# A fused LoRA kernel whose ScalarE copies B's rows on a semaphore of their own

## The chip, the core and the metric

The kernel runs on one core of one Trainium2 chip. The time is device microseconds of one execution, and each kernel's figure is the median of several executions. The engines of the core are TensorE (PE in the profile, with its weight loads as PEld), VectorE (DVE), ScalarE (ACT), GpSimd (POOL) and SyncE (SP), which here issues all transfers. Each engine works through its own program in order, and they meet only through semaphores: counters that one instruction raises and another waits for.

## The reference

```
x: 16 x 512 x 768 float32,  A: 768 x 16,  B: 16 x 768,  scale = 0.5
lora = np.matmul(np.matmul(x, A), B)
return (x + scale * lora).astype(np.float32)
```

x is 8192 rows of 768 numbers, 24 MB; the result is as large. A and B are small. The two products need little arithmetic, so most of what the kernel does is to bring x in, turn it so that TensorE can contract over the 768 columns, add the product, and bring the sum out.

## The kernel before, in words

The 8192 rows make 64 tiles of 128 rows, held on the chip as float32 in x_sb (48 tiles fit at once). They come in eight loads of 2, 6, 8, 8, 8, 16, 8 and 8 tiles and go out in five stores of 8, 8, 16, 16 and 16 tiles. Compute goes by **groups of eight tiles**, eight groups in all (g = 0 to 7). For each group:

- *Cast* (`narrowed`, line 196): x is copied to float16 into xn, the first four tiles of a group by ScalarE and the last four by GpSimd. Group 0 is cut finer: GpSimd casts its first two tiles, ScalarE the next two and then the last four. Before a cast an engine waits for the load that brought its tiles (lines 190 to 193) and for xn to be free again (line 195).
- *Turn* (`turned`, line 256): VectorE transposes xn in 32 x 32 blocks into xt.
- *Project* (`projected`, line 286): 24 matmuls of TensorE multiply xt with w_bd, the blocks of A, into the PSUM tile y_ps. The first lowers s_turned, the second raises **s_taken** (xt and xn of this group have been taken), the last raises s_y.
- *Spread* (line 241): ScalarE multiplies y_ps by the scale and writes it as four diagonal blocks into y_bd. The first of the four raises s_narrow, as the casts do; the last raises s_spread.
- *Raise* (`raised`, line 307): for each of the four pairs of tiles TensorE multiplies y_bd with b_mm, the rows of B, into one of the two PSUM tiles lora_ps, and raises s_lora.
- *Add* (`summed`, line 261): VectorE adds the lora_ps tile onto x_sb, in place. The stores take x_sb from there.

Casts and turns run a group ahead: during group g's raises, group g+1 is cast, turned and projected. TensorE's program has these groups as a loop (line 328); the other engines' programs are written out.

**B's rows** take a way of their own at the start. SyncE loads them spread over the partitions into b_rows (line 160). GpSimd casts them to float16 (b_half, line 214). Two matmuls of line 320 with the selection matrix pick put each row in the partitions where the raise wants it, into the first of the lora_ps tiles. ScalarE copies it out of PSUM into b_mm (line 234) and raises s_bm, for which TensorE waits ahead of its loop (line 327).

The order around the change: TensorE runs the two matmuls of line 320, waits for w_bd and for group 0's turn, and projects group 0 (line 326). ScalarE casts its parts of group 0, **waits for s_taken to reach 1** (line 233), copies b_mm, and then takes group 1's cast. Since it has already waited for s_taken at 1, ScalarE's cast of group 1 waits only for the load: that is why line 194 has `g > (e is nc.scalar)`, which is g > 1 for ScalarE and g > 0 for GpSimd.

SyncE's order: the two first loads, A, B, four more loads (lines 161 and 162), then a wait for the first two groups' sums and for ten raises (line 170), then the first two stores (lines 171 and 172). The last two loads each wait for one of these stores, because they go where its tiles lay. The later stores wait for the sums of their parts, and the third also for a raise of the sixth group (line 182). Once the sums are done GpSimd clears the semaphores (line 349), and the last store is issued after that (line 356).

Of the kernel before, what the change touches and what calls it, by code (L numbers as in the profile page):

```python
# [28 lines left out]
def kernel(  # L29
# [8 lines left out]
    nc = tc.nc  # L38
# [44 lines left out]
    def sem(name):  # L83
        sems.append(nc.alloc_semaphore(name))
        return sems[-1]
# [10 lines left out]
    def memory(t2, i, s, n):  # L96
        S = PARTS[i]
        return t2[ds(parts[i], S * P), :].rearrange("(p s) d -> p s d", s=S)[:, ds(s, n), :]

    def held(i, s, n):  # L100
        return tiles(where.index((i, s)), n)

    def tiles(t, n):
        return x_all[:, ds(t % ROOM, n), :]
# [6 lines left out]
    def load_of(t):  # L111
        i, s = where[t]
        return next(k for k, ld in enumerate(LOADS) if ld[0] == i and ld[1] <= s < ld[1] + ld[2])
# [1 line left out]
    assert SETS * SET == NC  # L115
    s_a, s_b = sem("s_a"), sem("s_b")
    s_ready, s_brows, s_pick = sem("s_ready"), sem("s_brows"), sem("s_pick")
    s_w, s_bh, s_bm = sem("s_w"), sem("s_bh"), sem("s_bm")
    s_first, s_narrow, s_turned, s_taken = sem("s_first"), sem("s_narrow"), sem("s_turned"), sem("s_taken")
    s_y, s_spread, s_lora = sem("s_y"), sem("s_spread"), sem("s_lora")  # L120

# [66 lines left out]
    def narrowed(e, copy, g, first, n=SUB):  # L188
        t = g * GROUP + first
        for k in dict.fromkeys(load_of(t + k) for k in range(n)):  # L190
            if (e, k) not in here:
                here.add((e, k))
                e.wait_ge(s_load[k], 16)
        if g > (e is nc.scalar):
            e.wait_ge(s_taken, g)
        ins = copy(out=xn[:, ds(first, n), :], in_=tiles(t, n))  # L196

        ins.then_inc(s_narrow if g else s_first if first else s_a, 1)

    def on_gpsimd(e):  # L200
        e.memset(a_rows[0:Q], 0.0).then_inc(s_ready, 1)  # L201
        e.memset(b_rows, 0.0).then_inc(s_brows, 1)  # L202
        e.memset(pick, 0.0).then_inc(s_pick, 1)
        e.memset(w_bd.rearrange("p c k m -> p (c k m)").bitcast(fp32), 0.0)  # L204
        e.memset(y_bd.rearrange("p s m -> p (s m)").bitcast(fp32), 0.0).then_inc(s_ready, 1)  # L205
        e.wait_ge(s_pick, 1)
        e.affine_select(  # L207
            out=pick, in_=pick, compare_op=mybir.AluOpType.not_equal, fill=1.0, base=0,
            pattern=[[0, NQ], [-APART, Q]], channel_multiplier=1,
        ).then_inc(s_pick, 1)  # L210
        narrowed(e, e.tensor_copy, 0, 0, SUB // 2)
        e.wait_ge(s_pick, 2)
        e.wait_ge(s_b, 16)
        e.tensor_copy(out=b_half, in_=b_rows).then_inc(s_bh, 1)  # L214
        e.wait_ge(s_ready, 3)
        e.tensor_copy(  # L216
            out=w_one.rearrange("i (c e) k r -> i c e (k r)", c=SETS),
            in_=a_t[0:Q].rearrange("i k r (e c) -> i c e (k r)", c=SET)[:, 0:SETS, 0:SET, :],
        ).then_inc(s_w, 1)
        e.wait_ge(s_w, 1)  # L220
        for b in range(NQ):
            e.tensor_copy(  # L222
                out=w_bd[ds(b * Q, Q), :, :, ds(b * Q, R)], in_=w_one
            ).then_inc(s_w, 1)
            e.wait_ge(s_w, b + 2)
        for g in range(1, NG):
            narrowed(e, e.tensor_copy, g, SUB)

    def on_scalar(e):
        narrowed(e, e.copy, 0, SUB // 2, SUB // 2)  # L230
        narrowed(e, e.copy, 0, SUB)

        e.wait_ge(s_taken, 1)
        e.copy(out=b_mm, in_=lora[0][:, 0, :]).then_inc(s_bm, 1)  # L234
        for g in range(NG):
            if g + 1 < NG:
                narrowed(e, e.copy, g + 1, 0)
            e.wait_ge(s_y, g + 1)
            for b in range(NQ):
                q = ds(b * Q, Q)  # L240
                last = e.mul(out=y_bd[q, :, q], in_=y_ps[q, :, :], mul=sc)  # L241
                if b == 0 and g + 1 < NG:

                    last.then_inc(s_narrow, 1)
            last.then_inc(s_spread, 1)
# [32 lines left out]
    def on_tensor(e):  # L278


        xv = xt.rearrange("p s (c j k) -> p s c j k", c=NC, k=2)

        def projected(first, last):
            for m in range(first, last):
                c, k = divmod(m, 2)
                mm = e.matmul(  # L286
                    y_ps, w_bd[:, c, k, :], xv[:, :, c, :, k],
                    start=(m == 0), stop=(m == MMS - 1),
                )
                if m == 0:  # L290
                    mm.then_inc(s_turned, -1)
                if m == 1:

                    mm.then_inc(s_taken, 1)
                if m == MMS - 1:
                    mm.then_inc(s_y, 1)

        def raised(p):
            if p == 0:
                e.wait_ge(s_spread, 1)  # L300
            free = s_free[(p + 2) % PAIRS]
            e.wait_ge(free, 1)
            t = lora[p % 2]
            mms = []
            for k in range(2):
                for n0, w in ((0, 512), (512, 256)) if k == 0 else ((0, 256), (256, 512)):
                    mms.append(e.matmul(  # L307
                        t[:, k, ds(n0, w)], y_bd[:, 2 * p + k, :], b_mm[:, ds(n0, w)],
                        start=True, stop=True,
                    ))  # L310
            if p == 0:
                mms[0].then_inc(s_raise, 1)
                mms[2].then_inc(s_spread, -1)
            mms[1].then_inc(free, -1)
            mms[-1].then_inc(s_lora, 1)

        e.wait_ge(s_pick, 2)
        e.wait_ge(s_bh, 1)
        for n0, w in ((0, 512), (512, 256)):
            last = e.matmul(  # L320
                lora[0][:, 0, ds(n0, w)], pick.rearrange("p b r -> p (b r)"),
                b_half[:, ds(n0, w)], start=True, stop=True,
            )
        e.wait_ge(s_w, 1 + NQ)
        e.wait_ge(s_turned, 1)
        projected(0, MMS)
        e.wait_ge(s_bm, 1)
        with e.Fori(0, NG - 1):
            raised(0)
            raised(1)  # L330
            e.wait_ge(s_turned, 1)
            projected(0, MMS // 2)
            raised(2)
            raised(3)
            projected(MMS // 2, MMS)
        for p in range(PAIRS):
            raised(p)

    on_sync(nc.sync)
    on_gpsimd(nc.gpsimd)  # L340
    on_scalar(nc.scalar)
    on_vector(nc.vector)
    on_tensor(nc.tensor)

    nums = [s.num for s in sems]
# [10 lines left out]
    last = nc.sync.dma_start(out=memory(out2, *STORES[-1]), in_=held(*STORES[-1]))  # L356
# [39 lines left out]
```

## Time and profile before

| | |
|---|---|
| median of 3 runs | 123.83 us (123.65 to 123.83) |
| profiled execution, its time | 123.56 us |
| its span, from first to last instruction | 121.6 us |
| busy: VectorE | 81.9 us (67%) |
| busy: TensorE matmuls | 51.1 us (42%) |
| busy: ScalarE | 37.4 us (31%), 43 instructions |
| busy: GpSimd | 28.4 us (23%) |
| moved by transfers | 50.43 MB, mean 415 GB/s |

How to read it: the span leaves out what lies before the first and after the last instruction, so the time is some 2 us longer. The profile shows one execution in three forms that matter here. The *slices* cut the span in 40 and give the busy share of each engine and of the 16 transfer engines in tenths. The *timeline* lists runs of like instructions: start, length, engine, line, operation, output and input; in brackets how long the engine had been idle, and which instruction ended that. The *windows* give for a stretch of the span each engine's busy time (with the number of instructions), the granted clock of TensorE, the transfers' share of their engines and their rate in GB/s. In short windows the transfers' share can come out above 1.00. Waits, semaphores and the issue of transfers do not count as busy.

### The profile page before, as it was taken

The page shows a single profiled execution, that of the slowest core. Times are in us where ns is not written, and L with a number is a line of the kernel's source. Part 1 is how long each engine was busy: PE and PEld are TensorE (multiplying, and loading weights), DVE is VectorE, ACT ScalarE, POOL GpSimd, SP SyncE. Part 2 cuts the span into 40 slices and gives each one's busy share as a digit, 9 for nine tenths or more (in the row PEclk, how much of TensorE's full clock was granted, in tenths as well). Part 3 has the DMA queues.
Part 4 walks back from the last instruction along what each step waited for, and adds up shares of the span by engine and source line. Part 5 has one row for each costly group of instructions (what it writes and reads, how often), then busy time and mean ns, then how long its engine had stood idle before and what let it go on. Part 6 is the DMA issues. An engine that isn't in the chain of part 4 may idle for free.

```text
span 121.6 us, 888 instructions
## 1 busy us (share of the span) xinstructions
PE 51.1 (42%) x322; PEld 29.9 (25%) x322; DVE 81.9 (67%) x42; ACT 37.4 (31%) x43; POOL 28.4 (23%) x24
## 2 busy tenths in 40 slices
PE   0000239477457457747745725894574520000000
PEld 0000026244233324424423412552342110000000
DVE  0002950799999999999999969999996992000000
ACT  4003919535417402826240093634004000000000
POOL 7731638135017002606200080620000000000000
PEclk9999999999999999999999998599999998555555
DMA  3999999999998997999999999998999899899890
GB/s 59 436 430 449 445 420 428 445 420 420 477 517 356 420 517 315 428 428 445 420 420 445 436 412 485 420 517 372 404 517 404 372 517 404 372 517 420 356 517 0
DMA packets 1928, 50.43 MB, mean 415 GB/s; under 512 B 236, under 2 KB 236, under 8 KB 392
## 3 DMA queue, kind: packets, MB, share of 16 engines
q1 hardware_dynamic: 1928, 50.43, 97.0%
HBM read 25.26 MB, written 25.17 MB: 415 GB/s over the span
## 4 chain that ended last, share of the span: by engine, by line
DVE 32%; DMA 29%; PE 12%; ACT 9%; issue 1%; SPq 0%; POOLq 0%
DMA x_sb<-in_x_dram 20%; DVE x_sb L261 19%; DVE xt L256 12%; DMA out_dram<-x_sb 9%; PE ps_yt L286 8%; ACT xn L196 6%; PE lora_ps L307 4%; ACT y_bd L241 3%; SPq L139 0%; SPq L391 0%; POOLq L134 0%; POOLq L377 0%
## 5 line engine op out<-in xcount | busy, mean ns | idle before, releaser
L261 DVE TENSOR_TENSOR x_sb<-x_sb,lora_ps 128x1536 f32<-128x1536 f32 x32 | 53.8, 1736 | 1.5 <-PE lora_ps L307 1.4
L307 PE MATMUL lora_ps<-b_mm,y_bd 128*128 128x512 f16 (+1 forms) x128 | 25.1, 329 | 22.2 <-ACT y_bd L241 14.8
L196 ACT CAST xn<-x_sb 128x3072 f16<-128x3072 f32 (+1 forms) x9 | 23.4, 2609 | 34.5 <-DMA x_sb<-in_x_dram 21.7
L286 PE MATMUL ps_yt<-xt,w_bd 128*128 128x256 f16 x192 | 26.5, 291 | 12.9 <-DVE xt L256 12.9
L256 DVE STREAM_TRANSPOSE xt<-xn 128x3072 f32<-128x3072 f32 (+1 forms) x9 | 27.1, 3007 | 6.6 <-ACT y_bd L241 6.1
L196 POOL CAST xn<-x_sb 128x3072 f16<-128x3072 f32 (+1 forms) x8 | 20.7, 2586 | 45.1 <-DMA x_sb<-in_x_dram 23.4
L286 PEld LDWEIGHTS ps_yt<-xt,w_bd 128*128 128x128 f16 x192 | 19.1, 102 | 21.1 <-issue 16.2
L307 PEld LDWEIGHTS lora_ps<-b_mm,y_bd 128*128 128x128 f16 x128 | 10.6, 97 | 34.8 <-ACT y_bd L241 17.0
L241 ACT ACTIVATE y_bd<-ps_yt 32x256 f16<-32x256 f32 x32 | 12.0, 374 | 18.1 <-PE ps_yt L286 17.7
L249 DVE STREAM_TRANSPOSE a_t<-a_rows 32x1024 f32<-32x1024 f32 x1 | 2.0, 1975 | 11.3 <-DMA a_rows<-in_A_dram 11.3
L320 PE MATMUL lora_ps<-b_half,pick 128*128 128x512 f16 (+1 forms) x2 | 0.8, 501 | 12.5 <-POOL b_half L214 12.5
L320 PEld LDWEIGHTS lora_ps<-b_half,pick 128*128 128x128 f16 x2 | 0.1, 105 | 12.5 <-issue 12.5
L222 POOL COPY w_bd<-w_one 32x384 f16<-32x384 f16 x4 | 2.0, 500 | 0.2
L214 POOL CAST b_half<-b_rows 128x768 f16<-128x768 f32 x1 | 0.8, 827 | 4.4 <-DMA b_rows<-in_B_dram 4.4
L234 ACT CAST b_mm<-lora_ps 128x768 f16<-128x768 f32 x1 | 0.8, 799 | 2.6 <-PE ps_yt L286 2.6
L196 ACT ACT_TABLE_LOAD x1 | 1.3, 1283 | 0.9 <-PEq L377 0.9
L204 POOL MEMSET w_bd<- 128x1536 f32 x1 | 1.4, 1372 | 0.0
L201 POOL MEMSET a_rows<- 32x1024 f32 x1 | 0.9, 941 | 0.5 <-POOLq L134 0.5
L216 POOL CAST w_one<-a_t 32x384 f16<-32x384 f32 x1 | 0.9, 851 | 0.9 <-DVE a_t L249 0.9
L202 POOL MEMSET b_rows<- 128x768 f32 x1 | 0.7, 727 | 0.0
L205 POOL MEMSET y_bd<- 128x512 f32 x1 | 0.5, 514 | 0.0
L207 POOL TENSOR_SCALAR_AFFINE_SELECT pick<-pick 128x128 f16<-128x128 f16 x1 | 0.3, 298 | 0.0
(5 smaller groups left out, 0.6 us busy)
## 6 DMA issues: line engine op xcount, KB each, us to landing
out_dram<-x_sb SPq DMA_DIRECT2D x3, 6144.0 KB, 19.0
x_sb<-in_x_dram SPq DMA_DIRECT2D x5, 3072.0 KB, 14.6
x_sb<-in_x_dram SPq DMA_DIRECT2D x1, 6144.0 KB, 41.7
out_dram<-x_sb SPq DMA_DIRECT2D x2, 3072.0 KB, 14.4
x_sb<-in_x_dram SPq DMA_DIRECT2D x1, 2304.0 KB, 9.9
x_sb<-in_x_dram SPq DMA_DIRECT2D x1, 768.0 KB, 4.7
a_rows<-in_A_dram SPq DMA_DIRECT2D x3, 16.0 KB
b_rows<-in_B_dram SPq DMA_DIRECT2D x1, 48.0 KB, 7.5
```

Of the source, the lines that this page charges most:

```text
L196: ins = copy(out=xn[:, ds(first, n), :], in_=tiles(t, n))
L201: e.memset(a_rows[0:Q], 0.0).then_inc(s_ready, 1)
L204: e.memset(w_bd.rearrange("p c k m -> p (c k m)").bitcast(fp32), 0.0)
L216: e.tensor_copy(out=w_one.rearrange("i (c e) k r -> i c e (k r)", c=SETS), in_=a_t[0:Q].rearrange("i k r (e c) -> i c e (k r)", c=SET)[:, ...
L222: e.tensor_copy(out=w_bd[ds(b * Q, Q), :, :, ds(b * Q, R)], in_=w_one).then_inc(s_w, 1)
L241: last = e.mul(out=y_bd[q, :, q], in_=y_ps[q, :, :], mul=sc)
L249: e.transpose(out=a_t[0:Q].rearrange("i k r c -> i (k r) c"), in_=a_rows[0:Q].rearrange("c (i k r) -> c (k r) i", k=2, r=R),).then_inc(s_r ...
L256: return e.transpose(out=ts[0], in_=ts[1])
L261: ins = e.tensor_tensor(out=xs, in0=xs, in1=lora[p % 2], op=mybir.AluOpType.add)
L286: mm = e.matmul(y_ps, w_bd[:, c, k, :], xv[:, :, c, :, k], start=(m == 0), stop=(m == MMS - 1),)
L307: mms.append(e.matmul(t[:, k, ds(n0, w)], y_bd[:, 2 * p + k, :], b_mm[:, ds(n0, w)], start=True, stop=True,))
L320: last = e.matmul(lora[0][:, 0, ds(n0, w)], pick.rearrange("p b r -> p (b r)"), b_half[:, ds(n0, w)], start=True, stop=True,)
```

## The change

ScalarE's copy of b_mm no longer waits for s_taken. A new semaphore, s_bp, is raised by TensorE's second matmul of line 320, ahead of the first projection, and the copy waits for that. ScalarE's cast of group 1 now waits for s_taken itself, as GpSimd's does. So one wait changes its semaphore, one is added to ScalarE's program, and one matmul has a semaphore to raise. No transfer and no arithmetic changes.

```diff
-    s_w, s_bh, s_bm = sem("s_w"), sem("s_bh"), sem("s_bm")
+    s_w, s_bh, s_bp, s_bm = sem("s_w"), sem("s_bh"), sem("s_bp"), sem("s_bm")
...
-        if g > (e is nc.scalar):
+        if g:
             e.wait_ge(s_taken, g)
         ins = copy(out=xn[:, ds(first, n), :], in_=tiles(t, n))
...
         narrowed(e, e.copy, 0, SUB // 2, SUB // 2)
         narrowed(e, e.copy, 0, SUB)
-
-        e.wait_ge(s_taken, 1)
+        e.wait_ge(s_bp, 1)
         e.copy(out=b_mm, in_=lora[0][:, 0, :]).then_inc(s_bm, 1)
...
                 lora[0][:, 0, ds(n0, w)], pick.rearrange("p b r -> p (b r)"),
                 b_half[:, ds(n0, w)], start=True, stop=True,
             )
+        last.then_inc(s_bp, 1)
         e.wait_ge(s_w, 1 + NQ)
```

## The prediction

> **What bounds the kernel now.** I read the page first: the forty slices, then the transfer queue's share.
>
> ```profile
> span 121.6 us, 888 instructions
> DVE  0002950799999999999999969999996992000000
> DMA  3999999999998997999999999998999899899890
> q1 hardware_dynamic: 1928, 50.43, 97.0%
> ```
>
> The transfer engines are at nine tenths or nearly so from the second slice to the second last, and their packets fill 97.0% of the span. VectorE is also full over a long stretch, but it falls silent in the last quarter, while the transfers run on. So the end is set by 50.43 MB that have to pass; an engine matters only if it makes the transfers wait. To see whether one can, I read SyncE's issues in the timeline, and beside them the windows around the change from loads to stores.
>
> ```profile
> 4.57 2.05 SPq L139 DMA_DIRECT2D x_sb<-in_x_dram  x4
> 44.15 0.82 SPq L149 DMA_DIRECT2D out_dram<-x_sb  x2
> 47.90 2.75 ACT L196 CAST xn<-x_sb 128x3072 f16<-128x3072 f32 x1 [5.30 <-DMA x_sb<-in_x_dram]
> 101.84 0.33 SPq L356 DMA_DIRECT2D out_dram<-x_sb  x1
> ```
>
> ```profile
> core 0: us, PE busy (x) PEld busy (x) DVE busy (x) ACT busy (x) POOL busy (x), PEclk, DMA share, GB/s
> 24.00:44.00 20.00, 12.65 (x85) 7.39 (x83) 20.00 (x11) 8.50 (x10) 5.49 (x2) 1.00 1.04 446
> 44.00:48.00 4.00, 2.44 (x17) 1.39 (x16) 4.00 (x3) 0.10 (x1) 0.07 (x1) 1.00 0.83 356
> 48.00:55.00 7.00, 3.63 (x24) 2.16 (x24) 7.00 (x4) 4.14 (x5) 2.67 (x1) 1.00 1.02 439
> 91.00:105.00 14.00, 4.05 (x25) 1.88 (x22) 8.79 (x6) 1.50 (x4) 0.00 (x0) 0.91 0.98 425
> ```
>
> The four loads of line 139 are issued by 6.62 us (4.57 + 2.05) and run on their own for some forty us. The first two stores are issued at 44.15, before the last of those loads has come in: ScalarE's cast at 47.90 is the one that this load releases. The first store therefore stands in the queue 47.90 − 44.15 = 3.75 us before the loads are over. Its start-up cost is not shown; the nearest row is the smallest load of x:
>
> ```profile
> x_sb<-in_x_dram SPq DMA_DIRECT2D x1, 768.0 KB, 4.7
> ```
>
> At 439 to 446 GB/s (the full windows' rate) 768 KB take 1.8 us, so of its 4.7 us at most 2.9 are start-up. The first store thus has between 3.75 − 2.9 = 0.85 us and 3.75 us to spare. This **cover of at least 0.85 us** is what any delay of the early chain must use up before the transfers feel it. At the last store (101.84) the window 91 to 105 shows a share of 0.98, so there is no gap there either.
>
> **The change, step by step.** It touches the start alone. These are the timeline's rows there:
>
> ```profile
> 11.24 4.13 ACT L196 CAST xn<-x_sb 128x1536 f16<-128x1536 f32 x2 [9.07 <-DMA x_sb<-in_x_dram]
> 12.55 0.80 PE L320 MATMUL lora_ps<-b_half,pick 128*128 128x512 f16 x2 [12.55 <-POOL b_half L214]
> 13.18 1.72 DVE L256 STREAM_TRANSPOSE xt<-xn 128x1536 f32<-128x1536 f32 x1
> 14.22 2.18 POOL L222 COPY w_bd<-w_one 32x384 f16<-32x384 f16 x4
> 15.40 1.78 DVE L256 STREAM_TRANSPOSE xt<-xn 128x1536 f32<-128x1536 f32 x1 [0.50 <-ACT xn L196]
> 17.33 4.42 PE L286 MATMUL ps_yt<-xt,w_bd 128*128 128x256 f16 x24 [3.98 <-DVE xt L256]
> 17.95 0.80 ACT L234 CAST b_mm<-lora_ps 128x768 f16<-128x768 f32 x1 [2.58 <-PE ps_yt L286]
> 18.76 2.75 ACT L196 CAST xn<-x_sb 128x3072 f16<-128x3072 f32 x1
> 18.85 2.74 POOL L196 CAST xn<-x_sb 128x3072 f16<-128x3072 f32 x1 [2.44 <-DMA x_sb<-in_x_dram]
> 21.79 1.54 ACT L241 ACTIVATE y_bd<-ps_yt 32x256 f16<-32x256 f32 x4 [0.28 <-PE ps_yt L286]
> 22.19 3.38 DVE L256 STREAM_TRANSPOSE xt<-xn 128x3072 f32<-128x3072 f32 x1 [5.01 <-ACT y_bd L241]
> ```
>
> *The copy of B moves.* Its source is ready when the two matmuls of line 320 end, at 12.55 + 0.80 = 13.35. ScalarE is then still casting group 0, until 11.24 + 4.13 = 15.37. So the copy goes from 17.95 to about 15.39, into ScalarE's idle 2.58 us, and ends near 16.2. It removes 0.80 us of work from 17.95 to 18.75. Beside it now lie VectorE's transpose at 15.40 and GpSimd's copies at 14.22. The transposes bound what that costs: the one at 13.18 ran beside ScalarE's and GpSimd's casts in 1.72 us, the one at 15.40 with ScalarE idle in 1.78. Company of this engine cost nothing there (−0.06), so I take 0. Should it cost 0.06 after all, that delays the projection by as much.
>
> *Group 1's cast doesn't move.* It was queued behind the copy and began at 18.76. Now two things hold it: the new wait, satisfied by the projection's second matmul as the copy's was (17.95), and the load of part 1. GpSimd's half of the same cast reads the same load, stood idle for 2.44 us, and started at 18.85 when the load had come. ScalarE's start at 18.76 says that the load was in by then, GpSimd's 18.85 that it wasn't long before. The gain of this cast is at most 0.80 (if the load came by 17.95) and at least 0; I take 0, because GpSimd's row names the load.
>
> *What follows doesn't move either way.* After the cast ScalarE waits 0.28 us more, for the projection's last matmul, before y_bd at 21.79. If the cast did start earlier, that idle would only grow. VectorE's transpose at 22.19 waits for y_bd, not for the cast. So the chain projection, y_bd, transpose is unchanged: **0 us**, with a cover of 0.28 us for anything that delays ScalarE here.
>
> *The added wait.* Behind it on ScalarE's queue stand group 1's cast and y_bd, and behind those VectorE, TensorE and the first store. The trace has no row for a bare wait. The nearest is a group where such a wait is already there:
>
> ```profile
> 25.72 1.50 PE L286 MATMUL ps_yt<-xt,w_bd 128*128 128x256 f16 x12 [0.86 <-DVE xt L256]
> 26.20 2.75 ACT L196 CAST xn<-x_sb 128x3072 f16<-128x3072 f32 x1 [2.87 <-PE ps_yt L286]
> ```
>
> From the start of the projection's first matmul to the cast are 0.48 us; in group 0 the same stretch to the copy was 17.95 − 17.33 = 0.62. With the wait in front, the release was no slower. The bounds are 0 and 0.48 us (were the whole release paid again); I take 0, since it is spent while the load is still out. At 0.48 it would exceed the 0.28 by 0.20, which the 0.85 at the first store still hides.
>
> *The added raise.* One matmul of line 320 now signals. Then TensorE stands idle for 3.98 us. The Trainium skill ("TensorE: Matmul & The Clock Gate", The cost: per-tile semaphore tail) prices one more signalling matmul at about 26 ns; by it the sum would still be 0, and no row here shows the price.
>
> *TensorE's wait for the copy* (line 327) is met earlier, but the next matmuls also need y_bd, so nothing gains. No transfer is added or moved past another, and SyncE's and GpSimd's orders stay. One more semaphore is cleared at line 349, ahead of the last store; the full window 91 to 105 hides it.
>
> **Sum:** 0 + 0 + 0 = 0 on a span of 121.6. The profiled execution took 123.56 with 1.96 around the span; the three runs' median is 123.83, with 123.65 to 123.83 among them, and the profile stands 0.27 below it. The forecast is the median, rounded: **123.8 us**. About 0.2% (0.25 us) is what a measurement of this kernel can tell from no change.
>
> **The rivals.** *Faster: the copy had disturbed the projection.* In the before kernel ScalarE reads PSUM beside the projection's matmuls. The 24 of them take 4.42 us, while 12 take 1.50 at 25.72, so 24 would take 3.00. If the copy were the cause, up to 1.42 us would come off the chain, and the first store would go out that much earlier. It could fill at most the thin stretch at 44 to 48: at its neighbours' (446 + 439) / 2 = 442 GB/s those 4 us would carry the same bytes in 3.22, so 0.78 us is lost there. That gives 123.83 − 0.78 = 123.05. Against it stand two windows:
>
> ```profile
> 18.00:18.80 0.80, 0.80 (x6) 0.52 (x5) 0.00 (x0) 0.79 (x2) 0.00 (x0) 1.00 1.07 461
> 18.80:19.60 0.80, 0.80 (x5) 0.56 (x4) 0.00 (x0) 0.80 (x1) 0.75 (x1) 1.00 0.86 369
> 20.40:21.20 0.80, 0.80 (x8) 0.60 (x7) 0.00 (x0) 0.80 (x1) 0.80 (x1) 1.00 1.00 430
> ```
>
> With the copy over, 18.8 to 19.6 is as slow as 18.0 to 18.8; the pace rises only past 20.4. The granted clock stands at 1.00 throughout, so the rows do not name the cause. The same page of the Trainium skill (The HAM clock gate) says that TensorE runs at half rate for its first 3.4 us or so of work; the pace here, rising some 3 us after 17.33, agrees, and by it nothing comes off. There remain smaller shifts in how the transfers mix. Chance 0.17 in all, and little of it at the full price.
>
> *Slower: the handover from loads to stores comes late.* Place: the first store at 44.15. VectorE is busy without a break from 22.19 until then, so whatever ScalarE loses past its 0.28 us at 21.79 is carried there undiminished. If the longer program makes ScalarE stall (to bring in code, say), by more than 0.28 + 0.85 = 1.13 us, the transfers run dry; that is the point from which it decides. I price it by the thin stretch coming twice: +0.78, so 124.6. The dear end is a stall as long as the smallest load, 4.7 us: 4.7 − 1.13 = 3.6, so 127.4. For it: the transfers are saturated, so a disturbance anywhere can only add, and the 0.85 us is a bound worked out from another transfer. Against it: no engine's row shows such a stall now, and the one queue in the profile carries x, A, B and out. The Trainium skill ("Runtime: NRT & Kernel Launch", Instruction fetch mechanics) has programs brought in by blocks of 256 instructions, with crossings mostly hidden; by it this program, 43 busy instructions and their waits, would not stall for one more, and the time would be the forecast's. Chance 0.27, most of it near the lower price or below.
>
> *The change does less than it says.* If the copy still began only after 17.9, the time would be the same again, 123.8; it is counted with the forecast.
>
> **How the numbers follow.** No change: 0.56, own range 123.6 to 124.05. Slower by over 0.2%: 0.27, at 124.1 to 124.6 for the most part, dear end 127.4. Faster by over 0.2%: 0.17, from 123.55 down to 123.05. The range reaches upward to the slower case's price and downward a third of the way to the faster one's: 123.4 to 124.6, leaving out some 0.2 (most of the full faster price, and the dear end).
>
> **What would show it.** In the changed kernel the copy of line 234 should start near 15.39, group 1's cast on ScalarE within 0.1 us of 18.76 and named as waiting for the load, y_bd after a wait for the projection of about 21.79, and the first store near 44.15, with transfers still at 97%. If y_bd comes over 0.5 us earlier, the projection was disturbed, and the faster rival holds. If a gap without a releaser opens on ScalarE and the first store moves past 45, the slower one does. If all starts agree and the time still differs by over 0.25 us, it lies in the transfers' own pace, which I have taken as fixed; that would be the error.

## The result

The changed kernel takes 123.47 us (median of 17 runs, 123.24 to 123.69) against 123.67 for the kernel before (17 runs, 123.49 to 124.11): a ratio of **0.9984, 95% interval 0.9978 to 0.9991**. That is 0.2 us, or 0.16%: less than the 0.2% that the prediction set as its bound, but clear of zero.

The profiled execution took 123.47 us with a span of 121.7. First the page of the changed kernel (span, the VectorE and transfer slices, the transfer queue):

```profile
span 121.7 us, 889 instructions
...
DVE  0002850599999999999999989999995991000000
...
DMA  3999999999998997999999999997998899799790
...
q1 hardware_dynamic: 1928, 50.43, 97.0%
```

One instruction more, and all else alike: the same 50.43 MB, the same 97.0%, and a span that is no shorter (121.7 against 121.6). Then the start, from its timeline. In the changed source the lines from the copy to the matmuls of line 320 have numbers one lower (234 is now 233, 256 is 255).

```profile
11.08 4.13 ACT L196 CAST xn<-x_sb 128x1536 f16<-128x1536 f32 x2 [8.91 <-DMA x_sb<-in_x_dram]
...
15.23 0.80 ACT L233 CAST b_mm<-lora_ps 128x768 f16<-128x768 f32 x1
15.24 1.78 DVE L255 STREAM_TRANSPOSE xt<-xn 128x1536 f32<-128x1536 f32 x1 [0.35 <-ACT xn L196]
...
17.16 5.14 PE L285 MATMUL ps_yt<-xt,w_bd 128*128 128x256 f16 x24 [3.82 <-DVE xt L255]
18.60 2.75 ACT L196 CAST xn<-x_sb 128x3072 f16<-128x3072 f32 x1 [2.57 <-DMA x_sb<-in_x_dram]
18.69 2.74 POOL L196 CAST xn<-x_sb 128x3072 f16<-128x3072 f32 x1 [2.31 <-DMA x_sb<-in_x_dram]
```

The copy has moved to the end of group 0's casts, and ScalarE's cast of group 1 now waits 2.57 us for its load. Both halves of that cast start 0.16 us earlier than in the profile before, ScalarE's and GpSimd's alike, because the loads came that much earlier in this execution (group 0's cast too: 11.08 against 11.24). So the cast gained nothing from the copy's move.

Where, then, are the 0.2 us? Not in the span. Each run gives its time and its span, so **time minus span** can be taken run by run. It averages 1.771 us over the changed kernel's 17 runs (1.73 to 1.82). For the kernel before, the one profiled execution shows 123.56 − 121.6 = 1.96 (with the unrounded span of the trace, 121.62, it is 1.94), and the 99 runs that stand beside the experiments average 1.933, 1.936 and 1.935 on three chips. The spans average 121.70 for the changed kernel and 121.67 to 121.70 for the one before. The 17 runs of the kernel before that gave the ratio have no spans on record, so this sets runs of different occasions side by side; e1 and e9 below repeat it with both kernels on one chip. By these figures 0.16 of the 0.20 us lie in what a profile's span leaves out, and the other 0.04 are within the scatter of the spans.

### The profile page after: what moved, and what is told of

The parts are those of the page before. It is cut to its first block, busy times and chain, and to the rows that moved or that the text cites. A ratio compares the mean times of both kernels' runs of the same rounds, so it can differ in the third digit from the quotient of the medians.

```text
span 121.7 us, 889 instructions
## 1 busy us (share of the span) xinstructions
PE 50.7 (42%) x322; PEld 29.6 (24%) x322; DVE 81.7 (67%) x42; ACT 37.4 (31%) x43; POOL 28.4 (23%) x24
## 2 busy tenths in 40 slices
DMA packets 1928, 50.43 MB, mean 414 GB/s; under 512 B 236, under 2 KB 236, under 8 KB 392
## 3 DMA queue, kind: packets, MB, share of 16 engines
q1 hardware_dynamic: 1928, 50.43, 97.0%
## 4 chain that ended last, share of the span: by engine, by line
DVE 34%; DMA 28%; PE 10%; ACT 9%; issue 1%; SPq 0%; POOLq 0%
DVE x_sb L260 22%; DMA x_sb<-in_x_dram 20%; DVE xt L255 12%; DMA out_dram<-x_sb 8%; PE ps_yt L285 6%; ACT xn L196 6%; PE lora_ps L306 3%; ACT y_bd L240 3%; SPq L139 0%; SPq L391 0%; POOLq L134 0%; POOLq L377 0%
```

## The experiments

Three theories were put against each other. **L**: the part outside the span depends on how many instructions ScalarE's program has. **C**: the copy's early place saves the time. **S**: one more semaphore does. All edits below are to the kernel before unless said otherwise. A "satisfied wait" is a wait for a value that is already reached, so that it costs a place in the program and no waiting. An instruction has room for one wait of its own, and only a further wait ahead of it is an instruction more: e11 adds 28 waits in its source, but 16 instructions (904 in its profile against 888), because 12 of the waits go with multiplications that had none. In e12 the copy and its wait go as one instruction. The number of instructions in each profile confirms that each edit added what it was meant to.

| kernel | ScalarE's length | ratio to before (95%) | time minus span, mean of runs | span, mean |
|---|---|---|---|---|
| e12 | −1 | 1.0008 (0.9998 to 1.0019) | 2.131 (12 runs) | 121.61 |
| before, on the three chips | 0 | | 1.933, 1.936, 1.935 (99) | 121.68, 121.70, 121.67 |
| e3, the same kernel again | 0 | 1.0004 (0.9995 to 1.0013) | 1.935 (11) | 121.71 |
| e2 | 0 | 1.0000 (0.9991 to 1.0009) | 1.951 (11) | 121.65 |
| the change | +1 | 0.9984 (0.9978 to 0.9991) | 1.771 (17) | 121.70 |
| e1 | +1 | 0.9990 (0.9981 to 0.9999) | 1.778 (11) | 121.70 |
| e9 | +1 | 0.9987 (0.9977 to 0.9996) | 1.788 (12) | 121.68 |
| e4 | +2 | 1.0001 (0.9991 to 1.0010) | 1.856 (11) | 121.74 |
| e10 | +2 | 0.9987 (0.9977 to 0.9997) | 1.858 (12) | 121.62 |
| e5 | +3 | 1.0006 (0.9994 to 1.0018) | 1.94 (10) | 121.71 |
| e6 | +4 | 0.9998 (0.9985 to 1.0011) | 1.89 (10) | 121.76 |
| e11 | +16 | 0.9993 (0.9982 to 1.0004) | 1.783 (12) | 121.75 |

Means of ten or so runs are good to about 0.01 us outside the span (0.03 for e5 and e6, which spread) and to 0.02 to 0.05 for the span itself. The spans are listed to 0.1 us, and that rounding alone lets a single run's time minus span vary by 0.1. So the outside part tells kernels apart that the whole time hardly does.

**e1: the added wait alone.**

```diff
-        if g > (e is nc.scalar):
+        if g:
```

> The copy of b_mm stays where it was, behind s_taken; only ScalarE's second wait of the change is made (for s_taken at 1 ahead of group 1's cast, already satisfied there). No new semaphore. Theory L (the gain of 0.20 us lies outside the span and comes from ScalarE's program being one instruction longer): time minus span 1.77 us as in the changed kernel, against 1.96 (123.56 less 121.6) in the profiled execution of before; ratio to before 0.9984. Theory C (the gain comes from the copy's early place): time minus span 1.95, ratio 1.000. Theory S (from one more semaphore): ratio 1.000.

1.778 us, ratio 0.9990. The copy is as late as before in its timeline, yet the gain is there:

```profile
17.80 0.80 ACT L234 CAST b_mm<-lora_ps 128x768 f16<-128x768 f32 x1 [2.58 <-PE ps_yt L286]
18.74 2.75 ACT L196 CAST xn<-x_sb 128x3072 f16<-128x3072 f32 x1
```

**e2: the copy alone, the length kept.** The changed kernel with, in place of its two waits at group 1:

```diff
-                e.wait_ge(s_load[k], 16)
-        if g:
-            e.wait_ge(s_taken, g)
+                e.wait_ge(s_load[k], 16 + (g == 1))
+        if g > 1:
+            e.wait_ge(s_taken, g - 1)
+        elif g and e is nc.gpsimd:
+            e.wait_ge(s_w, 1 + NQ)
...
-        projected(0, MMS)
+        projected(0, MMS, s_load[2])
```

(the last argument is the semaphore that the second matmul raises in place of s_taken).

> The copy waits for s_bp and is early, as in the change, with the new semaphore, but ScalarE's program is as long as before: the first projection's second matmul raises the semaphore of group 1's load, and group 1's casts wait for 17 there in one wait instead of for load and s_taken in two. GpSimd gets a satisfied wait in exchange, so that its length stays too. Theory L: time minus span 1.95 us, ratio to before 1.000. Theory C: ratio 0.9984, gain inside the span. Theory S: 1.77, ratio 0.9984.

1.951 us, ratio 1.0000. Its timeline has the copy early and the cast after its load, as in the change:

```profile
15.30 0.80 ACT L235 CAST b_mm<-lora_ps 128x768 f16<-128x768 f32 x1
18.62 2.75 ACT L198 CAST xn<-x_sb 128x3072 f16<-128x3072 f32 x1 [2.52 <-PE ps_yt L287]
```

(the wait is put down to the matmul, which raises the same semaphore as the load). With the copy early and s_bp there, nothing is gained. C and S fall, since each had expected the gain here.

**e3: the kernel before, again.** No edit.

> The kernel before, unchanged, as a kernel of its own, so that the span of each of its runs is listed. All theories: ratio 1.000 with an interval of some 0.001 to either side. L and S: time minus span 1.95 us in every run, spans as in the changed kernel's runs (121.7). C: time minus span 1.77 in most runs and spans 0.2 longer than the changed kernel's.

1.935 us, span 121.71, ratio 1.0004: the outside part is steady, and the comparison has no bias that it could show.

**e4: two more.** The edit of e1, and

```diff
             e.wait_ge(s_y, g + 1)
+            if g == 0:
+                e.wait_ge(s_taken, 1)
```

> The kernel before with two more satisfied waits on ScalarE (group 1's for s_taken at 1 as in e1, and one more ahead of the first y_bd), nothing else. If each instruction of length takes 0.18 us off: time minus span 1.59, ratio 0.997. If it is the evenness of the length: back to 1.95, ratio 1.000. If one instruction passes some boundary: 1.77, ratio 0.9984. Theories C and S: 1.95, ratio 1.000.

1.856 us, a value that none of the three readings of L had named: neither one step further nor back. The dependence is on length, but not a straight one.

**e5 and e6: three and four more.** As e4, with `if g < 2` and `if g < 3`.

> The kernel before with three more satisfied waits on ScalarE (group 1's cast, the first two groups' y_bd). So far time minus span was 1.93 us at +0, 1.78 at +1, 1.86 at +2, spans alike. If every instruction past a boundary costs 0.08 and the boundaries stand four apart: 1.93 or 1.94 at +3. If evenness plays in: 1.78 again. If only the total length past one boundary counts and the 0.08 is chance: 1.78 to 1.86. Were it the place of the wait and not the length: any.

> The same with four more waits (group 1's cast, the first three groups' y_bd). Repeating every four instructions: 1.93 us as at +0. Rising by 0.08 each past one boundary: 2.02. Repeating every three: 1.78. Span as before, 121.7.

On average 1.94 and 1.89, but with a new spread: single runs lie between 1.76 and 2.09 (e5) and 1.78 and 2.02 (e6), where the kernels above stay within 0.1. The profile shows something new too. This is the transfer view of e5 from 121.6 to 126, past the span's end; its 40 slices are 0.11 us each:

```profile
DMA  0000000000000000200000000000000000000000
GB/s 0 0 0 0 0 0 0 0 0 0 0 0 0 0 0 0 74 0 0 0 0 0 0 0 0 0 0 0 0 0 0 0 0 0 0 0 0 0 0 0
DMA packets 1, 0.01 MB, mean 2 GB/s; under 512 B 0, under 2 KB 0, under 8 KB 0
## 3 DMA queue, kind: packets, MB, share of 16 engines
q14 instruction: 1, 0.01, 0.5%
```

One packet on a queue of its own kind, *instruction*: a block of code (8192 bytes in the trace's record) fetched in the seventeenth slice, at 121.6 + 16 × 0.11 = 123.36 us, 1.9 us after the last instruction of this execution's span of 121.5 us. The view counts it where it starts; it lasts some 0.35 us (0.5% of 16 engines over 4.4 us). In e1 the same view is empty:

```profile
DMA  0000000000000000000000000000000000000000
GB/s 0 0 0 0 0 0 0 0 0 0 0 0 0 0 0 0 0 0 0 0 0 0 0 0 0 0 0 0 0 0 0 0 0 0 0 0 0 0 0 0
DMA packets 0, 0.00 MB, mean 0 GB/s; under 512 B 0, under 2 KB 0, under 8 KB 0
```

One reading is that code runs behind the span, that its place in ScalarE's code moves with the program's length, and that at +3 it reaches a mark where a further block is fetched. But the time of this execution was 123.48 us. Even if all that lies outside its span lay behind it, the fetch, from 123.36 to some 123.7 us, would still end after the time does. That the time waits for the fetch is therefore not shown; fetch and spread only appear at the same lengths.

**e7 and e8: one more on another engine.** VectorE and GpSimd:

```diff
             e.wait_ge(s_lora, g * PAIRS + p + 1)
+            if g == p == 0:
+                e.wait_ge(s_first, 2)
```

```diff
         e.wait_ge(s_ready, 3)
+        e.wait_ge(s_pick, 2)
```

> The kernel before with one more satisfied wait on VectorE, ahead of its first add; ScalarE as before. If the time outside the span hangs on ScalarE's length alone: 1.93 us, ratio 1.000. If on every engine's, by the slowest: 1.93 or another value between 1.75 and 2.05, span 121.7 in either case.

> The kernel before with one more satisfied wait on GpSimd, ahead of the cast into w_one, which lies 0.8 us off the chain through ScalarE and VectorE; ScalarE as before. ScalarE's length alone: 1.93 us, ratio 1.000. Every engine's: another value between 1.75 and 2.05, span 121.7.

1.926 and 1.938 us with spans of 121.71 and 121.74, ratios 1.0001 (0.9990 to 1.0012) and 1.0006 (0.9994 to 1.0017). Of the engines tried, one instruction more counts on ScalarE alone. Other lengths of VectorE's and GpSimd's programs weren't tried, and TensorE and SyncE not at all.

**e9: one more, at the other end of the program.**

```diff
             e.wait_ge(s_y, g + 1)
+            if g == NG - 1:
+                e.wait_ge(s_taken, 1)
```

> The kernel before with one satisfied wait more on ScalarE, ahead of the last group's y_bd, at the other end of its program from e1. So far time minus span: 1.93 us at +0, 1.78 at +1, 1.86 at +2, and 1.94 and 1.89 with much spread at +3 and +4, where the profile shows 8 KB of code loaded after the span's end. If only the number of instructions counts: 1.78, ratio to before 0.999. If it is what the wait does at the start: 1.93, ratio 1.000. Span 121.7 either way.

1.788 us, ratio 0.9987, as e1 and as the change. At one instruction more it doesn't matter where it stands or what it waits for: the number counts.

**e10: the change and one more.** The edit of e4's second part on the changed kernel.

> The changed kernel (copy early, s_bp) with one more satisfied wait on ScalarE ahead of the first y_bd, so two longer than before. Length alone: time minus span 1.86 us as in e4, against the change's 1.77; ratio to before about 0.9995. If the early copy is worth something by itself: 1.77 kept, or a shorter span than 121.7, ratio 0.9984.

1.858 us, e4's value, so with the copy early as with the copy late the outside part goes by the length. The expected ratio was 0.9995; 0.9987 was measured, because the spans of these runs average 121.62, within their scatter. By the ratio alone this kernel would pass for the change.

**e11: sixteen more.**

```diff
                 q = ds(b * Q, Q)
+                if g < 4:
+                    if b:
+                        e.wait_ge(s_y, g + 1)
+                    e.wait_ge(s_taken, 1)
```

> The kernel before with sixteen satisfied waits more on ScalarE, ahead of the y_bd multiplications of the first four groups. If the time outside the span is a matter of a block of code that is loaded when the program's end passes a mark: the load comes earlier than the 1.7 to 1.9 us after the span's end seen in e5 and e6, by the time of some twelve instructions, is seen in the profile, and has less of the end waiting for it: 1.75 to 1.95, with less spread than at +3 and +4. If each instruction counts by itself, at 0.08 us or so: over 2.5. Span 121.7 to 121.9.

1.783 us with as little spread as e1, and span 121.75. The block of code is now fetched inside the span. This is its transfer view from 82.06 to 82.10:

```profile
DMA packets 1, 0.01 MB, mean 205 GB/s; under 512 B 0, under 2 KB 0, under 8 KB 0
## 3 DMA queue, kind: packets, MB, share of 16 engines
q14 instruction: 1, 0.01, 48.3%
```

At that moment ScalarE has begun group 6's y_bd:

```profile
81.93 1.55 ACT L245 ACTIVATE y_bd<-ps_yt 32x256 f16<-32x256 f32 x4 [2.06 <-PE ps_yt L290]
91.84 1.54 ACT L245 ACTIVATE y_bd<-ps_yt 32x256 f16<-32x256 f32 x4 [8.37 <-PE ps_yt L290]
```

Here ScalarE has nearly forty us of its program still ahead, and the fetch costs nothing that shows: y_bd takes 1.55 us around it and 1.54 in the next group, and the time outside the span is as small as e1's. Read as the same fetch as in e5, it has been moved by thirteen instructions from 1.9 us behind the span to forty us before its end.

**e12: one fewer.** e2 with the copy of b_mm taken from ScalarE to VectorE:

```diff
         ins.then_inc(s_turned, 1)
+        e.wait_ge(s_bp, 1)
+        e.tensor_copy(out=b_mm, in_=lora[0][:, 0, :]).then_inc(s_bm, 1)
```

> ScalarE one instruction shorter than before: VectorE makes the copy of b_mm in its idle stretch ahead of group 1's turn (5.0 us idle in before), and group 1's casts wait once, as in e2. VectorE is one longer, which changed nothing in e7 (1.93). If the length has the shape of steps of 0.08 past a mark, the next lower value: 1.85. If the mark lies between +0 and +1 only: 1.93. If the time outside grows as the program's end moves away from the mark: 2.0. Span 121.7, since the copy lies in idle time.

2.131 us, the worst of all, above any value that was expected; the span stays (121.61), since the copy lies in VectorE's idle time:

```profile
16.89 0.92 DVE L271 CAST b_mm<-lora_ps 128x768 f16<-128x768 f32 x1
```

VectorE's program is longer here as well; e7 says that one instruction more there does nothing by itself. The value at −1 rests on this one kernel.

**What is shown and what stays open.** Shown: the part of the time outside the span goes by the number of ScalarE's instructions, and not by where an added wait stands or what it waits for (e1, e9 and the change agree within 0.02 us; e4 and e10 within 0.01; before, e3 and e2 within 0.02). In the profiled executions a further block of code is fetched near the end at +3 and +4, and early at +16, where it costs nothing that shows. Not shown: why −1, 0, +1 and +2 give 2.13, 1.93, 1.78 and 1.86, since in these no fetch stands in the record near the end. That the closing code's position against the next block sets these values is a guess from the fetch at +3. Nor does any run here show whether the outside part lies ahead of the span or behind it; only that the fetch lies behind.

No version beats the change: no length tried has less outside the span than +1 (+16 equals it within the noise), and e1 and e9 reach +1 with a wait that does nothing.

## Why the prediction was right, and which step failed

The time lies in the range, and the ratio within the bound that counted as no change; but the forecast of zero was off by 0.2 us, and for a reason that none of its cases held. There was luck in it. 123.47 us is 0.07 above the range's lower end, outside the 123.6 to 124.05 that the case of no change had for itself, and among the times of the faster case, whose mechanism did not occur. Of the 0.33 us between it and the forecast of 123.8, 0.20 are the gain; the other 0.13 come from the start of the sum, a median of three runs (123.83) where 17 runs give 123.67.

**The transfers as the bound, and the first store's cover: held, and tested harder than meant.** In the changed kernel's profile y_bd starts at 22.34, not near 21.79, and the first store at 44.70, not 44.15:

```profile
22.34 1.55 ACT L240 ACTIVATE y_bd<-ps_yt 32x256 f16<-32x256 f32 x4 [0.99 <-PE ps_yt L285]
```

```profile
44.70 0.82 SPq L149 DMA_DIRECT2D out_dram<-x_sb  x2
47.74 2.75 ACT L196 CAST xn<-x_sb 128x3072 f16<-128x3072 f32 x1 [4.59 <-DMA x_sb<-in_x_dram]
```

The change isn't the cause: y_bd waited for the first projection, which was slower. That projection took 5.14 us here, 4.42 in the profile before, 4.18 in e3's, which is the same kernel, and 5.10 in e1's, where the copy is late:

```profile
17.06 4.18 PE L286 MATMUL ps_yt<-xt,w_bd 128*128 128x256 f16 x24 [3.93 <-DVE xt L256]
```

```profile
17.18 5.10 PE L286 MATMUL ps_yt<-xt,w_bd 128*128 128x256 f16 x24 [3.72 <-DVE xt L256]
```

The moment at which TensorE's pace rises differs between executions. The trace itself, below the views printed here, records it. In the profile before, the projection's matmuls start some 213 ns apart up to 20.70 us and 110 to 115 ns apart from there on, and 20.70 is where the trace's first entry of the granted clock, at full rate, begins. In e3's profile this entry begins at 19.93 us, in e1's at 21.97 and in the changed kernel's at 22.03: the later it comes, the longer the projection. The windows print 1.00 ahead of that entry too, where the trace has none; that is why the prediction found no cause in its rows. The Trainium skill ("TensorE: Matmul & The Clock Gate", The HAM clock gate) says that the window by which the clock is raised runs freely and doesn't start with the kernel; this spread agrees. The delay of 0.55 us at the first store cost the span nothing that shows (121.6 and 121.7 us), as the cover of at least 0.85 said. The changed kernel's windows show the handover no thinner and the stretch behind it nearly as full, while around the last store the share is 0.94, against 0.98 before:

```profile
44.00:48.00 4.00, 2.51 (x20) 1.49 (x18) 4.00 (x3) 0.26 (x1) 0.23 (x1) 1.00 0.86 369
48.00:55.00 7.00, 4.11 (x28) 2.25 (x25) 7.00 (x4) 3.99 (x5) 2.51 (x1) 1.00 0.99 425
91.00:105.00 14.00, 3.72 (x22) 1.60 (x19) 8.46 (x6) 1.50 (x4) 0.00 (x0) 0.84 0.94 407
```

**The copy: right.** Foretold for 15.39, right behind group 0's casts; found at 15.23, behind casts that end at 11.08 + 4.13 = 15.21. The turn beside it took 1.78 us in both kernels, so its company cost nothing that shows.

**Group 1's cast and what follows: right.** The load holds the cast, and the profile now says so by name (2.57 us). That y_bd comes after the projection's last matmul is right too; that it stays near 21.79 is not, because the projection's length isn't fixed.

**The added wait and the raise: right inside the span** (121.70 us on average, against 121.67 to 121.70), wrong as a sum. The added wait was priced between 0 and 0.48 us by what a wait does where it stands. Its price was 1.77 − 1.93 = −0.16 us, for being one instruction more in the program, and outside the span.

**The step that failed is the one that carried the time from the span to the execution:** "The profiled execution took 123.56 with 1.96 around the span". It took those 1.96 us for a constant of the kernel. They average 1.93 before and 1.77 after, and no other term of the sum moved by more than its scatter. The prediction's closing sentence made the transfers' own pace the place to look for a difference of over 0.25 us with all starts as foretold. The difference stayed below that, and the sentence has the same fault: it leaves out the time around the span, while the transfers' share is 97.0% in both.

**The faster rival** (the copy had disturbed the projection) falls: without the copy beside it the projection was slower, not faster, its pace goes by the clock's entry, and e2 gains nothing. **The slower rival** named the loading of code by ScalarE, inside the span and as a loss. It would have to stop ScalarE there for over 1.13 us, and the sign given for it, a first store past 45 us, did not come (44.70). When a block is fetched inside the span (e11), nothing stops. The Trainium skill ("Runtime: NRT & Kernel Launch", Instruction fetch mechanics) calls such crossings mostly hidden, and e11 agrees. The prediction gave its blocks as 256 instructions; each late fetch on record here is one packet of 8192 bytes, and how many instructions that holds no run shows. Near the program's end, e5 and e6 have 1.76 to 2.09 us outside the span, which may be a crossing that isn't hidden; as said above, that is not shown.

## What to carry to other kernels

A profile's span is not the time: take time minus span run by run as a term of its own, for it is steadier (0.03 us from run to run here) than the span (0.1), and a difference of 0.1% between two kernels may sit there alone. Before a gain that small is put down to the edit's idea, pad the old kernel with an instruction that does nothing: if that gains as much, the idea has gained nothing, and the next edit to that engine can lose it again (here 1.78 us at one instruction more became 1.86 at two). In a kernel that transfers fill, 0.55 us of delay in a chain that has 0.85 to spare cost nothing that the span shows.

## What the runs showed of the hardware

- The time outside the span depended on the number of instructions in ScalarE's program: 2.13, 1.93, 1.78, 1.86 us at −1, 0, +1 and +2, and one instruction more on VectorE or GpSimd left it alone (1.93 and 1.94). Why it takes these values stays open.
- With ScalarE's program longer, one more block of code (8192 bytes) was fetched late, on a queue of its own: at 123.36 us, 1.9 us behind the end of the span, with three instructions more, and at 82.1 us with sixteen more. Inside the span it cost nothing that the runs can tell (121.75 against 121.67 us, each good to some 0.04).
- The first projection's 24 matmuls took 4.18 us (e3) to 5.28 us (e4) in executions of programs whose TensorE instructions are the same. They started some 213 ns apart until the trace's first entry of the granted clock, and 109 to 115 ns apart after it; that entry began at 19.93 us in e3 and at 22.71 us in e4.
